# Attention: sums stored ahead of the heads, four places for them, a bfloat16 mask row, reciprocals as 128x16, filler beside the last products

## The chip, the core and the metric

The kernel runs on one core of one Trainium2 chip. A core has a matrix engine (PE, with its weight loads shown apart as PEld), a vector engine (DVE), a scalar engine (ACT), a general engine (POOL), and a queue from which transfers are issued (SP). Each of them works through its own list of instructions in order and waits for semaphores that the others raise. The metric is device microseconds of one execution; the time of a kernel is the median of several executions.

## The reference

One layer of a hybrid decoder block on x of 2048 x 1024 (float32): a root-mean-square norm, one input projection, three mixers that read the same projection, and one output projection that is added to x. The attention mixer is the part that the change touches: 8 heads of 64, causal, with a cumulative forget gate in the exponent.

```python
q = rms_norm(q, q_g); k = rms_norm(k, k_g); c = cumsum(log_f)
logits = q @ k.T * scale + (c_q[:, None] - c_k[None, :])
logits = where(kpos <= qpos, logits, -inf)
p = softmax(logits);  o = p @ v            # per head, then * silu(z_att)
mix = concat([y_att, y_ssd, y_lru])        # 512 + 1024 + 512 columns
h = h + mix @ w_out
```

The other two mixers are a chunked state-space scan (SSD) and a gated linear recurrence (LRU). Products are made to float32 accuracy by splitting each operand into a high and a low part and adding three products.

## The kernel before

**Order.** The program is traced in one order, and a planner then makes the list of every engine from it: it simulates the program and gives an engine, among the instructions whose operands and buffer places are ready in the simulation, the one that stands first in the traced order (a block with `high_priority` counts as traced earlier; `issue_after` keeps a block behind a given instruction). So the traced order is a preference and not the order itself, and a small edit can move many instructions after it. A buffer pool with `bufs=n` has n places for a tag; the next tile of the tag waits until the oldest place has been read.

**Stages.** From 0 to about 1257 us the norm, the projections, the convolutions, the LRU and the SSD run; all results go to DRAM tensors. From there to about 1862 us attention runs (`score`, `av`, `finish`), with pieces of the output projection laid between as filler. After that only output projection is left.

**Attention.** `units` holds 64 pairs (head, block of 256 queries); the first head goes through its blocks downward, the others upward, so that each head from the second on starts with short units. `tasks` holds a unit's key blocks of 256, 288 in all. For task i the loop at L1324 calls `score` (two pairs of products into a PSUM tile T, on the diagonal a mask product; ACT's exponential twice, L1069 and L1070, DVE's difference L1071, POOL's running sum of the exponentials), `av` of task i - 3 (L1114 to L1116, accumulated in O), and, where that ends a unit, `finish`. `maxima` prepares the next unit: row minima of the logits on DVE (L1022 with the mask `zm` on the diagonal chunk, L1027 elsewhere, joined at L1025), which `flip` (L1040 to L1042) puts as a row into q. `load_head` loads a head's keys and values, 2.6 MB.

**What finish does.** Two small products add up the exponentials (L1124, L1125). ACT copies the upper half of O to `to` (L1128) and the row of sums to `su` (L1129, three places), DVE joins `to` (L1130, L1131), POOL multiplies with the gate into `za` (L1132, five places). One task later `store` sends `za` to `at_d` (L1138) and `su` to `s_d` (L1139). After the last head of a block the sums of all 8 heads of 256 positions come back as `sr` of 16 x 128 (L1145, one place), DVE takes the reciprocal (L1146), `r_d` is stored (L1147), and four tasks later the block is marked ready. `later(f, n)` runs f n tasks on.

**Filler.** `sweeps` is a generator over the output projection; a step is three products of 512 columns (L1192 to L1194), four steps are a `half`, which DVE adds to the running result (L1198, L1200). Within attention all halves share one PSUM bank (`psP`). After each `score` the loop calls `fill`, which lets the generator go on to `FIRST + count * RATE // 288` steps, 12 + 290 after the last of 288 tasks, each step behind marks on PE, ACT and DVE four tasks back. In the last three turns of the loop there is no score, so no `fill`. Then the attention's PSUM pools are closed, and the rest of the generator runs with six banks. `mix` loads a block of attention output and the reciprocals (`rb`, L1168).

All these transfers are issued on SP, in one list.

Of the kernel before, what the change touches and what calls it, by code (L numbers as in the profile page):

```python
# [8 lines left out]
F32 = mybir.dt.float32  # L9
F32R = mybir.dt.float32r  # L10
I32 = mybir.dt.int32
BF16 = mybir.dt.bfloat16
# [6 lines left out]
P = 128  # L19
# [19 lines left out]
AVL = 3  # L39
# [10 lines left out]
def hybrid_block(ctx, tc, x, norm_g, w_in, q_norm_g, k_norm_g, forget_b, ssd_conv_w, ssd_conv_b,  # L50
# [3 lines left out]
    def tpool(**kw):  # L54
        if kw.get("space") is not DRAM:
            kw["reuse_waits"] = "tile"
        return tc.tile_pool(**kw)

    V, A, G, T = nc.vector, nc.scalar, nc.gpsimd, nc.tensor
    dma = nc.sync.dma_start  # L60
# [8 lines left out]
    def dram(name, shape, dt=F32):  # L69
        return dp.tile(shape, dt, name=name, tag=name)  # L70
# [12 lines left out]
    s_d = dram("s_d", [NT, 8, P])  # L83
    r_d = dram("r_d", [NT, 8, P])
    gt_d = [dram(f"gt_d{g}", [4, P, S]) for g in range(2)]
    at_d = dram("at_d", [4, P, S])
# [135 lines left out]
    with tpool(name="p0", bufs=2) as p0, tpool(name="p01", bufs=1) as p01, \  # L222
# [81 lines left out]
        for tb in range(4):  # L304
            if tb + AHEAD < 4:
                norm_x(tb + AHEAD)
            for k in range(KD):
                pt, tag = ((psY, "Y"), (pst, "pt"))[(tb * KD + k) % 5 % 2]
# [11 lines left out]
            if tb == 0:  # L320
# [5 lines left out]
                j = CV["cw"]  # L326
                V.tensor_scalar(cv[:, j:j + 60], cv[:, j:j + 60], 0.5, None, op0=ALU.mult)
                j = CV["qg"]
                V.tensor_scalar(cv[:, j:j + 1], cv[:, j:j + 1], -0.125, None, op0=ALU.mult)
                j = CV["ba"]  # L330
                V.tensor_scalar(cv[:, j:j + 4], cv[:, j:j + 4], -1.0, None, op0=ALU.mult)
                j = CV["bx"]
# [180 lines left out]
    with tpool(name="cl", bufs=1) as cl, tpool(name="g1", bufs=1, side="right") as g1:  # L513
        for gq in range(6):
# [5 lines left out]
            if gq == 3:  # L520
                ll = cl.tile([P, 4], F32, name="ll")
                j = CV["lam"]
# [265 lines left out]
    def load_head(h):  # L788
        p, b = divmod(h, 2)
        hs = slice(b * 64, b * 64 + 64)  # L790
        pool = kvB if b else kvA
        k2 = k2s[b]
        kx = pool.tile([P, S], F32R, name=f"kx{h}", tag="kx")

        vv = pool.tile([P, NT, 130], F32R, name=f"vv{h}", tag="vv")
        dma(k2[0:64, :].bitcast(F32), qk_d["k", "h", p][hs, :])
        dma(k2[64:66, :].bitcast(F32), c_d[h].rearrange("i t l -> i (t l)"))
        dma(kx[0:64, :].bitcast(F32), qk_d["k", "l", p][hs, :])
        dma(kx[64:128, :].bitcast(F32), qk_d["k", "h", p][hs, :])
        dma(vv[:, :, 0:128].bitcast(F32), v_d[:, h, :].rearrange("(t p) c -> p t c", p=P))  # L800
        G.memset(vv[:, :, 128:130].bitcast(F32), 1.0)
        heads[h] = k2, kx, vv

    def load_q(j):
        h, sb = units[j]
        p, b = divmod(h, 2)
        hs = slice(b * 64, b * 64 + 64)
        q3, qx = q3s[j // 2 % 3], qxs[j // 2 % 3]
        sb -= sb % 2
        qs = slice(sb * 256, sb * 256 + 512)  # L810
        dma(q3[0:64, :].bitcast(F32), qk_d["q", "h", p][hs, qs])
        dma(qx[0:64, :].bitcast(F32), qk_d["q", "h", p][hs, qs])
        dma(qx[64:128, :].bitcast(F32), qk_d["q", "l", p][hs, qs])
        qs_[j // 2] = q3, qx

    kc = kvA = kvB = zm = onr = idr = zmt = None
# [3 lines left out]
    def make_q(pool):  # L820
        i = len(q3s)
        q3 = pool.tile([P, 512], F32R, name=f"q3{i}")
        G.memset(q3[64:128, :].bitcast(F32), 0.0)
        G.memset(q3[64:66, :].bitcast(F32), 1.0)
        q3s.append(q3)
        qxs.append(pool.tile([P, 512], F32R, name=f"qx{i}"))

    def make_k2(b):
        k2 = (kvB if b else kvA).tile([P, S], F32R, name=f"k2{b}")
        G.memset(k2[64:128, :].bitcast(F32), 0.0)  # L830
        G.memset(k2[96:97, :].bitcast(F32), -1.0)
        k2s[b] = k2

    def begin():

        nonlocal kc, kvA, zm, onr, idr, zmt
        sx.close()
        sgx.close()
        kc = cx.enter_context(tpool(name="kc", bufs=1, side="right"))
        kvA = cx.enter_context(tpool(name="kvA", bufs=1, side="right"))  # L840

        zm = kc.tile([P, 640], F32, name="zm")
        G.memset(zm, 0.0)
        G.affine_select(out=zm[:, 512:640], in_=zm[:, 512:640], pattern=[[-1, P]],
                        compare_op=ALU.is_ge, fill=-NEG, base=0, channel_multiplier=1)

        onr = kc.tile([P, 65], F32R, name="onr")
        G.memset(onr[:, 0:64].bitcast(F32), 0.0)
        G.memset(onr[:, 64:65].bitcast(F32), 1.0)
        idr = kc.tile([P, P], F32R, name="idr")  # L850
        V.tensor_copy(idr, ident)
        zmt = kc.tile([P, P], F32R, name="zmt")
        V.tensor_scalar(zmt, tri, NEG, -NEG, op0=ALU.mult, op1=ALU.add)
        for i in range(2):
            make_q(kc)
        make_k2(0)
        load_head(0)
        load_q(0)
# [111 lines left out]
    a1 = cx.enter_context(tpool(name="a1", bufs=1))  # L970
    a2 = cx.enter_context(tpool(name="a2", bufs=2))
    a3 = cx.enter_context(tpool(name="a3", bufs=3))
    a4 = cx.enter_context(tpool(name="a4", bufs=4))
# [125 lines left out]
    def av(j, kp):  # L1099


        h, sb = units[j]
        u = U[j]
        vv = heads[h][2]
        if kp == 0:
            u["O"] = psO.tile([P, 512], F32, name=f"O{j}", tag="O")
        po = u["O"]
        ph, pl = u.pop(kp)
        for jj in range(2):
            kt = kp * 2 + jj  # L1110
            qs = slice(P if kp == sb and jj else 0, 256)
            cs = slice(256 * jj, 256 * jj + 256 - qs.start)
            q2 = slice(256 + qs.start, 512)
            T.matmul(po[:, qs], vv[:, kt, 0:128], ph[:, cs], start=(kt == 0),  # L1114
                     stop=(kt == 2 * sb + 1), skip_group_check=True)
            T.matmul(po[0:65, q2], vv[:, kt, 64:129], pl[:, cs], start=False, stop=False,  # L1116
                     skip_group_check=True)

    def finish(j):

        h, sb = units[j]
        u = U[j]
        po = u["O"]
        T.matmul(po[0:65, 256:512], onr, u["ah"], start=False, stop=False, skip_group_check=True)  # L1124
        T.matmul(po[0:65, 256:512], onr, u["al"], start=False, stop=True, skip_group_check=True)  # L1125
        to = a2.tile([64, 256], F32, name=f"to{j}", tag="to")
        su = a3.tile([1, 256], F32, name=f"su{j}", tag="su")
        A.copy(to, po[64:128, 0:256])  # L1128
        A.copy(su, po[64:65, 256:512])  # L1129
        V.tensor_tensor(to, po[0:64, 0:256], to, op=ALU.add)  # L1130
        V.tensor_tensor(to, po[0:64, 256:512], to, op=ALU.add)  # L1131
        G.tensor_tensor(u["za"], to, u["za"], op=ALU.mult)  # L1132
        p, b = divmod(h, 2)
        cs = slice(sb * 256, (sb + 1) * 256)
        qt = slice(sb * 2, sb * 2 + 2)

        def store():
            dma(at_d[p][b * 64:b * 64 + 64, cs], u["za"])  # L1138
            dma(s_d[qt, h:h + 1, :].rearrange("i o t -> o i t"),  # L1139
                su.rearrange("o (i t) -> o i t", i=2))  # L1140
            if h < 7:
                return

            sr = a1.tile([16, P], F32, name=f"sr{j}", tag="sr")
            later(lambda: dma(sr, s_d[qt].rearrange("i h t -> (i h) t")), 2)  # L1145
            later(lambda: V.reciprocal(sr, sr), 4)  # L1146
            later(lambda: dma(r_d[qt].rearrange("i h t -> (i h) t"), sr), 5)  # L1147
            later(lambda: ready.add(sb), 8)

        later(store, 1)  # L1150


# [55 lines left out]
    def later(f, n=2):  # L1208

        if clock[0] is None:  # L1210
            f()
        else:
            late.append((clock[0] + n, f))

    def run_late(t):
        clock[0] = t
        while True:
            due = [z for z in late if t is None or z[0] <= t]
            if not due:
                return  # L1220
            due = min(due, key=lambda z: z[0])
            late.remove(due)
            due[1]()
# [80 lines left out]
    def fill(ins):  # L1304
        count[0] += 1
        marks["P"].append(ins)
        want = FIRST + count[0] * RATE // 288
        while want > count[1]:
            with ExitStack() as behind:
                for m in marks.values():  # L1310
                    behind.enter_context(tc.issue_after(m[max(0, len(m) - 1 - LAG)].ins))
                if next(filler):
                    break
            count[1] += 1

    tasks = [(j, kp) for j, (h, sb) in enumerate(units) for kp in range(sb + 1)]
    begin = [tasks.index((j, 0)) for j in range(len(units))]
    at = {}
    for j in range(1, len(units)):
        a, b = max(0, begin[j - 1] - LT), begin[j] - LT  # L1320
# [3 lines left out]
    for i in range(len(tasks) + AVL + 1):  # L1324
        ins = None
        run_late(i)
        if i < len(tasks):
            ins = score(*tasks[i])
            for f in at.get(i, ()):
                f()  # L1330
        if 0 <= i - AVL < len(tasks):
            av(*tasks[i - AVL])
        if i > AVL:
            j, kp = tasks[i - AVL - 1]
            if kp == units[j][1]:
                finish(j)
        if ins is not None:
            fill(ins)
# [36 lines left out]
```

## Time and profile before

| | us |
|---|---|
| median of 3 runs | 2002.28 |
| lowest, highest | 1999.08, 2002.97 |
| profiled execution | 2005.07 |
| its span, first to last instruction | 2003.4 |
| PE busy in the span | 1945.2 |
| DVE, ACT, POOL busy | 1287.7, 1004.3, 804.5 |

The span is what the profile divides up; the profiled execution is 1.7 us longer than it, and 2.8 us above the median of the runs. PE is the engine with the most work by far. A row of the timeline gives start, duration, engine, line and operation, the output and inputs by the program's names, and in brackets how long the engine had been idle and what it waited for. Pipelined products overlap in their records: products of 512 columns start 0.23 us apart at full clock although each is shown with 0.39.

### The profile page before, as it was taken

To read this page: it belongs to the slowest core of one execution; us is meant where nothing else is said; L and a number is where in the kernel's file an instruction comes from. 1 tells how busy PE (TensorE), PEld (TensorE's weight loads), DVE (VectorE), ACT (ScalarE), POOL (GpSimd) and SP (SyncE) were. 2 spreads that over 40 slices of the span, in tenths; PEclk is the share of its full clock that TensorE was granted. 3 is DMA by queue.
4 is the path that set the end of the run, shared out by engine and by line. 5 is a ranking of instruction groups with operands and counts; after the bars stand their busy time and mean duration, and the time that the engine had idled before them with its cause. 6 is when DMAs were issued, how large, how long until landed. Compare 5 with 4: busy or idle time off the path is not lost.

```text
span 2003.4 us, 34852 instructions
## 1 busy us (share of the span) xinstructions
PE 1945.2 (97%) x11941; PEld 1705.6 (85%) x11941; DVE 1287.7 (64%) x2573; ACT 1004.3 (50%) x2174; POOL 804.5 (40%) x920
## 2 busy tenths in 40 slices
PE   8999999999999999999999999999999999998999
PEld 6898888888989899888987897888899788987787
DVE  6738555573736465766566554788788787897433
ACT  6624444362535354444444433576777676775110
POOL 0100000131323233343443520787888688886110
PEclk9999999999999999999999999999999999999999
DMA  5232223111212134657646555764665754722453
GB/s 191 67 116 66 67 69 111 53 55 53 65 43 70 37 103 139 173 177 202 195 147 200 177 135 179 213 174 150 170 164 183 195 154 135 191 64 85 149 173 126
DMA packets 260032, 261.30 MB, mean 130 GB/s; under 512 B 26724, under 2 KB 198016, under 8 KB 258304
## 3 DMA queue, kind: packets, MB, share of 16 engines
q1 hardware_dynamic: 259696, 259.05, 44.1%
q8 instruction: 95, 1.56, 0.3%
q0 software_dynamic: 160, 0.03, 0.1%
q14 instruction: 81, 0.66, 0.1%
HBM read 164.22 MB, written 94.77 MB: 129 GB/s over the span
## 4 chain that ended last, share of the span: by engine, by line
PE 82%; DMA 6%; DVE 6%; ACT 3%; issue 2%; POOL 1%; SPq 1%; DVEq 0%; POOLq 0%; ACTq 0%
PE po L1192 6%; PE po L1194 5%; PE po L1193 5%; PE pxx L372 4%; PE pxx L373 4%; PE pxx L374 4%; PE pzs L358 3%; PE pzs L356 3%; PE pzs L360 3%; PE T L1058 3%; PE T L1059 3%; PE S L1017 3%; PE O L1114 3%; PE O L1116 3%; PE py L727 2%
## 5 line engine op out<-in xcount | busy, mean ns | idle before, releaser
L1071 DVE TENSOR_TENSOR pl<-T,ph 128x512 fp32r<-128x512 f32 (+1 forms) x288 | 185.8, 653 | 44.6 <-ACT T L1070 40.0
L1192 PE MATMUL po<-woh,mh 128*128 128x512 f32 x512 | 204.1, 399 | 0.5 <-DVE xr L1200 0.4
L1193 PE MATMUL po<-wol,mh 128*128 128x512 f32 x512 | 202.2, 395 | 0.0
L1194 PE MATMUL po<-woh,ml 128*128 128x512 f32 x512 | 201.9, 395 | 0.0
L1069 ACT ACTIVATE ph<-T 128x512 fp32r<-128x512 f32 (+1 forms) x288 | 165.4, 574 | 55.9 <-PE T L1059 48.1
L1084 POOL TENSOR_TENSOR ac<-ac,ph 128x512 f32<-128x512 f32 x120 | 157.6, 1313 | 22.5 <-ACT ph L1069 17.6
L1070 ACT ACTIVATE T<-T 128x512 f32<-128x512 f32 (+1 forms) x288 | 164.6, 571 | 0.3
L1058 PE MATMUL T<-q,k 128*128 128x256 f32 x576 | 147.2, 281 | 8.6 <-ACT q L1042 6.6
L356 PE MATMUL pqk<-wh,uh 128*128 128x256 f32 x512 | 155.3, 304 | 0.0
L372 PE MATMUL pxx<-uh,wh 128*128 128x512 f32 x384 | 153.7, 403 | 1.3 <-ACT uh L317 1.3
L373 PE MATMUL pxx<-ul,wh 128*128 128x512 f32 x384 | 153.1, 399 | 0.0
L374 PE MATMUL pxx<-uh,wl 128*128 128x512 f32 x384 | 150.9, 395 | 0.0
L1114 PE MATMUL O<-ph,vv 128*128 128x256 f32 (+1 forms) x576 | 148.6, 279 | 0.7 <-ACT ph L1069 0.7
L1027 DVE TENSOR_REDUCE mc<-S 128x1 f32<-128x512 f32 x192 | 128.5, 682 | 32.4 <-PE S L1017 30.8
L358 PE MATMUL pqk<-wl,uh 128*128 128x256 f32 x512 | 145.1, 284 | 0.8 <-DVE wl L210 0.8
L710 ACT ACTIVATE ab<-ab,nacs 128x128 f32<-128x128 f32 x256 | 82.8, 392 | 125.6 <-POOL ab L706 125.2
L435 DVE SCALAR_TENSOR_TENSOR accx<-rtx,cv,accx 128x512 f32<-128x512 f32 x144 | 108.1, 752 | 57.8 <-ACT accx L432 54.9
L360 PE MATMUL pqk<-wh,ul 128*128 128x256 f32 x512 | 144.2, 282 | 0.0
L358 PE MATMUL pzs<-wl,uh 128*128 128x256 f32 x512 | 143.6, 281 | 0.0
L360 PE MATMUL pzs<-wh,ul 128*128 128x256 f32 x512 | 143.3, 280 | 0.0
L356 PE MATMUL pzs<-wh,uh 128*128 128x256 f32 x512 | 143.0, 281 | 0.0
L1116 PE MATMUL O<-pl,vv 128*65 128x256 f32 x576 | 141.4, 278 | 1.5 <-DVE pl L1071 1.5
(357 smaller groups left out, 5743.3 us busy)
## 6 DMA issues: line engine op xcount, KB each, us to landing
ab<-acs_d SPq DMA_DIRECT2D x64, 256.0 KB
pt_d<-xr SPq DMA_DIRECT2D x64, 256.0 KB
wr<-in_w_in_dram SPq DMA_DIRECT2D x112, 128.0 KB
xt<-in_x_dram SPq DMA_DIRECT2D x16, 512.0 KB
xs_d<-stx SPq DMA_DIRECT2D x32, 256.0 KB
v_d<-vs SPq DMA_DIRECT2D x32, 256.0 KB
wr<-in_w_in_dram SPq DMA_DIRECT2D x128, 64.0 KB
zs_d<-zs SPq DMA_DIRECT2D x32, 256.0 KB
```

The source lines that it names most:

```text
L356: T.matmul(ps[:, i, :], h[k][:, sl], wh[k], start=(k == 0 and i == 0), stop=False, skip_group_check=True)
L358: T.matmul(ps[:, i, :], h[k][:, sl], wl[k], start=False, stop=False, skip_group_check=True)
L360: ins = T.matmul(ps[:, i, :], l[k][:, sl], wh[k], start=False, stop=last, skip_group_check=True)
L372: T.matmul(ps, wh[k][:, ms], uh[tb][k], start=(k == 0), stop=False)
L373: T.matmul(ps, wh[k][:, ms], ul[tb][k], start=False, stop=False)
L374: ins = T.matmul(ps, wl[k][:, ms], uh[tb][k], start=False, stop=(k == KD - 1))
L1058: T.matmul(ps, k2[:, ks], q3[:, qs], start=(jj == 0), stop=False, skip_group_check=True)
L1114: T.matmul(po[:, qs], vv[:, kt, 0:128], ph[:, cs], start=(kt == 0), stop=(kt == 2 * sb + 1), skip_group_check=True)
L1116: T.matmul(po[0:65, q2], vv[:, kt, 64:129], pl[:, cs], start=False, stop=False, skip_group_check=True)
L1192: T.matmul(ps, mh[:, j, :], h, start=(j == 0), stop=False)
L1193: T.matmul(ps, mh[:, j, :], l, start=False, stop=False)
L1194: T.matmul(ps, ml[:, j, :], h, start=False, stop=(j == 3))
```

## The change

The mask `zm` is held in bfloat16. `su` has four places instead of three. `store` sends the sums first, and the head's part `za` one task later than before. The 16 x 128 sums come back as 128 rows of 16, and go back in the same shape. `av` returns its last instruction, so that the last three turns of the loop, which have no score, call `fill` too, with the product's instruction as the mark: 291 calls instead of 288.

```diff
-        zm = kc.tile([P, 640], F32, name="zm")
+        zm = kc.tile([P, 640], BF16, name="zm")
...
-            T.matmul(po[0:65, q2], vv[:, kt, 64:129], pl[:, cs], start=False, stop=False,
-                     skip_group_check=True)
+            ins = T.matmul(po[0:65, q2], vv[:, kt, 64:129], pl[:, cs], start=False, stop=False,
+                           skip_group_check=True)
+        return ins
...
-        su = a3.tile([1, 256], F32, name=f"su{j}", tag="su")
+        su = a4.tile([1, 256], F32, name=f"su{j}", tag="su")
...
+        def flat(z):
+            return z.rearrange("i h (a b) -> (i h a) b", b=16)
+
         def store():
-            dma(at_d[p][b * 64:b * 64 + 64, cs], u["za"])
             dma(s_d[qt, h:h + 1, :].rearrange("i o t -> o i t"),
                 su.rearrange("o (i t) -> o i t", i=2))
+            later(lambda: dma(at_d[p][b * 64:b * 64 + 64, cs], u["za"]), 1)
             if h < 7:
                 return
-            sr = a1.tile([16, P], F32, name=f"sr{j}", tag="sr")
-            later(lambda: dma(sr, s_d[qt].rearrange("i h t -> (i h) t")), 2)
+            sr = a1.tile([P, 16], F32, name=f"sr{j}", tag="sr")
+            later(lambda: dma(sr, flat(s_d[qt])), 2)
             later(lambda: V.reciprocal(sr, sr), 4)
-            later(lambda: dma(r_d[qt].rearrange("i h t -> (i h) t"), sr), 5)
+            later(lambda: dma(flat(r_d[qt]), sr), 5)
...
-            av(*tasks[i - AVL])
+            ins = av(*tasks[i - AVL]) if ins is None else (av(*tasks[i - AVL]), ins)[1]
```

## The prediction

> **What bounds the kernel now.** I read the page's first part, then the table by windows for attention, then the waits and timelines of PE inside it.
>
> ```profile
> PE 1945.2 (97%) x11941; PEld 1705.6 (85%) x11941; DVE 1287.7 (64%) x2573; ACT 1004.3 (50%) x2174; POOL 804.5 (40%) x920
> ```
>
> ```profile
> 1257.30:1862.00 604.70, 586.27 (x3789) 522.39 (x3790) 487.72 (x1137) 420.06 (x956) 474.34 (x523) 0.99 0.55 156
> ...
> 1558.00:1634.00 76.00, 71.67 (x456) 63.70 (x455) 59.48 (x143) 50.92 (x116) 56.22 (x62) 0.96 0.60 165
> 1786.00:1862.00 76.00, 67.17 (x406) 57.88 (x405) 57.96 (x115) 43.48 (x96) 52.99 (x55) 0.96 0.31 91
> ```
>
> The columns are the stretch, its length, busy time with counts of PE, PEld, DVE, ACT, POOL, then granted clock, DMA share and GB/s. PE bounds: it is idle for 604.7 - 586.3 = 18.4 us in attention, the only stage that the change reaches. Of the stretches of one head, that from 1558 and the last one lose 4.3 and 8.8 us and show a lower clock; all others together lose 5.3. No edit removes a product, so the change can only win idle time and halved clock. Three places hold most of it.
>
> The first is at 1570 (PE, ACT and SP by the timeline):
>
> ```profile
> 1574.04 0.58 PE L1058 MATMUL T<-q,k 128*128 128x256 f32 x1 [3.46 <-ACT q L1042]
> 1575.07 0.63 PE L1192 MATMUL po<-woh,mh 128*128 128x512 f32 x1
> ```
>
> ```profile
> 1557.93 0.36 ACT L1129 COPY su<-O 1x256 f32<-1x256 f32 x1
> ...
> 1563.43 0.36 ACT L1129 COPY su<-O 1x256 f32<-1x256 f32 x1
> 1573.08 0.36 ACT L1129 COPY su<-O 1x256 f32<-1x256 f32 x1 [4.18 <-DMA s_d<-su]
> 1573.47 0.26 ACT L1041 CAST q<-T 1x128 fp32r<-1x128 f32 x1
> ```
>
> ```profile
> 1557.62 0.54 SPq L800 DMA_DIRECT2D vv<-v_d  x1
> 1558.26 7.99 SPq L1251 DMA_DIRECT2D pt_d<-xr  x1
> 1568.79 0.60 SPq L1139 DMA_DIRECT2D s_d<-su  x1
> ```
>
> A head's load has filled the transfers; SP is held for 7.99 us by the store behind it, so the sums of three short units wait for their issue. All three places of `su` are full, ACT waits 4.18 us for the first to land, and `flip`'s copies stand behind it, for which PE waits.
>
> The second is the end of attention:
>
> ```profile
> 1854.62 0.33 PE L1116 MATMUL O<-pl,vv 128*65 128x256 f32 x1 [1.27 <-DVE pl L1071]
> 1855.71 0.48 PE L1124 MATMUL O<-ah,onr 128*65 128x256 f32 x1 [0.64 <-ACT ah L1095]
> 1856.51 0.48 PE L1125 MATMUL O<-al,onr 128*65 128x256 f32 x1 [0.33 <-POOL al L1096]
> 1856.79 0.63 PE L1192 MATMUL po<-woh,mh 128*128 128x512 f32 x1
> 1859.25 0.39 PE L1192 MATMUL po<-woh,mh 128*128 128x512 f32 x1
> 1859.94 0.39 PE L1192 MATMUL po<-woh,mh 128*128 128x512 f32 x1
> ```
>
> The third is the chain of sums and reciprocals in the last head (PE, DVE, and the chain of waits):
>
> ```profile
> 1804.76 0.79 PE L1017 MATMUL S<-k,q 96*128 96x512 f32 x1 [2.21 <-DVE mc L1027]
> 1815.01 0.36 PE L1058 MATMUL T<-q,k 128*128 128x256 f32 x1 [1.73 <-DVE mz L1025]
> 1838.23 0.35 PE L1040 MATMUL T<-ident,mz 128*97 128x128 f32 x1 [0.92 <-DVE mz L1025]
> ```
>
> ```profile
> 1802.55 1.56 DVE L1170 TENSOR_TENSOR mt<-mt,rb 128x512 f32<-128x512 f32 x1 [1.53 <-DMA rb<-r_d]
> 1813.38 0.94 DVE L1146 RECIPROCAL sr<-sr 16x128 f32<-16x128 f32 x1 [3.22 <-DMA sr<-s_d]
> 1837.21 0.94 DVE L1146 RECIPROCAL sr<-sr 16x128 f32<-16x128 f32 x1
> ```
>
> Each time DVE waits for a transfer of this chain (1.53, 3.22) or works on a reciprocal (0.94), and the minima for which PE waits stand behind that in DVE's list.
>
> **The price of a halved clock.** After the 3.46 us wait, products of 512 columns take 0.63 instead of 0.39. Two stretches of the table by windows give the clock:
>
> ```profile
> 1574.00:1579.30 5.30, 5.26 (x16) 4.39 (x16) 2.57 (x7) 1.96 (x4) 1.87 (x3) 0.51 0.70 202
> 1856.80:1859.20 2.40, 2.40 (x7) 1.92 (x7) 1.53 (x3) 0.63 (x2) 0.56 (x1) 0.52 0.56 201
> 1804.70:1807.90 3.20, 3.14 (x10) 2.46 (x11) 3.02 (x8) 0.43 (x3) 0.00 (x0) 0.50 0.20 56
> ```
>
> 5.26 us at 0.51 is 2.6 us lost, 2.40 at 0.52 is 1.2, 3.14 at 0.50 is 1.6.
>
> **Part by part.**
>
> *Four places for the sums.* The fourth copy was due at 1573.08 - 4.18 = 1568.9 and finds a place; a fifth would have to come before the first landing at 1573.08, and the units after the short ones are longer. The wait on PE goes, 3.46 + 2.6 = 6.1 us. What is late next: the held SP list, which also carries q loads and gate loads; that is a rival. Bounds: 0 (another wait takes over) and -6.1. I take -6.1, since the row names `su`'s store and nothing else on ACT is due in those 4.18 us.
>
> *Filler beside the last products.* Three more calls make 12 + 291 * 290 // 288 = 305 steps instead of 302. A step takes 1859.94 - 1859.25 = 0.69 us, three 2.07. PE idles 1.27 + 0.64 + 0.33 = 2.24 in those turns and then loses 1.2 at half clock; the products moved there are gone from the full stretch behind. Against it: the planner already reaches over the loop's end.
>
> ```profile
> L1192 PE MATMUL po<-woh,mh 128*128 128x512 f32 x304 | 122.7, 404 | 0.5 <-DVE xr L1200 0.4
> 1852.47 0.67 DVE L1200 TENSOR_TENSOR xo<-xo,po 128x256 f32<-128x256 f32 x2
> ```
>
> Up to 1856.6 it had issued 304 steps, 76 whole halves, though the loop had asked for 302 and begun the last of them: the rest of a half that has its bank can be drawn ahead. The new half needs that bank emptied by DVE first, which ended at 1853.1 (L1200), so it can't start before the waits and lies where PE idles. I take 2.0 of the idle time and half of the clock's price: -2.6. Bounds 0 and -3.4. The Trainium skill, page "TensorE: Matmul & The Clock Gate", section "Why this matters for your kernels", asks for no idle gap above about 3 us, as one idle window halves the clock. Here the clock halved after a gap of 2.21 us and after 2.24 us in three pieces, so the measured rows decide; by the page the tail would be worth 2.0 and the sum would end 0.6 us higher.
>
> *Reciprocals as 128x16.* The rows by shape:
>
> ```profile
> L1146 DVE RECIPROCAL sr<-sr 16x128 f32<-16x128 f32 x8 | 7.5, 940 | 8.7 <-DMA sr<-s_d 8.5
> L144 DVE RECIPROCAL spf_d<-spf_d 128x128 f32<-128x128 f32 x1 | 0.9, 947 | 0.0
> L144 DVE RECIPROCAL spl_d<-spl_d 128x4 f32<-128x4 f32 x1 | 0.2, 178 | 0.0
> ```
>
> The partitions don't count, the elements in a row do: (947 - 178) / 124 = 6.2 ns each, so 16 take 252 ns. DVE wins 8 * 0.69 = 5.5 us. Of the eight only that at 1837.21 stands ahead of an instruction for which PE waits (0.92): -0.7. The others lie beside PE's work. The bounds are 0 and -0.9; if the cover goes, each is worth up to 0.69. Against it stand the transfers: a row of 64 bytes instead of 512. No row here is of this form.
>
> ```profile
> 1804.17 1.52 DMA sr<-s_d
> ...
> 1809.22 2.54 DMA r_d<-sr
> ```
>
> I take the landing as unchanged (1.5 and 2.5 us, mostly fixed: a row of 8 KB takes it); bounds are that and twice that. The Trainium skill, page "DMA: Bandwidth & Descriptors", section "Specifications", says that transfers below 512 bytes per piece fall off line rate and are read and written back; no run here shows it. It is a rival below.
>
> *Sums first, heads one task later.* The two stores of one unit already go in this order, as here:
>
> ```profile
> 1847.99 0.60 SPq L1139 DMA_DIRECT2D s_d<-su  x1
> 1850.02 0.49 SPq L1138 DMA_DIRECT2D at_d<-za  x1
> SPq L1002 <- DMA at_d<-za: 66.2, 45, 5.0
> ```
>
> The heads move by a task, 604.7 / 288 = 2.1 us. They hold one of five places of `za`, and SP waits for such a store in front of the next gate load already 45 times. Behind a waiting gate load stand q loads and sums. I take 0, since the gate is needed only in `finish`, units later; bounds 0 and the slower rival. The reads of `at_d` are let go only at the mark eight tasks on, which the new time doesn't reach.
>
> *Mask in bfloat16.* 128 instructions read it.
>
> ```profile
> L1022 DVE CUSTOM_DVE_ANT_0 jk<-S,zm 128x512 bf16<-128x512 f32 x32 | 21.9, 685 | 3.4 <-PE S L1017 2.4
> L1027 DVE TENSOR_REDUCE mc<-S 128x1 f32<-128x512 f32 x192 | 128.5, 682 | 32.4 <-PE S L1017 30.8
> ```
>
> The reduction without a mask takes as long, so the second operand costs nothing now: 0, bounded by 128 * 3 ns either way on DVE.
>
> *New order.* The planner lays attention out anew. The waits of 2.21 and 1.73 and a dozen under 0.7 are accidents of its order; some will go and others come. As an allowance I charge one new wait of the middle size, +1.7; bounds: -5.5 (2.21 + 1.6 + 1.73 gone) and +5.5 (as much again).
>
> **The sum.** 2003.4 - 6.1 - 2.6 - 0.7 + 1.7 = 1995.7 of span, 1997.4 with the 1.7 us around it, against 2005.07 of the same execution: 0.9962. On the median of the runs, 2002.28, that is 1994.6; I say 1995.
>
> **The rivals.**
>
> *Another wait takes the sums' place.* SP stays held for 7.99 us, and ACT, freed, meets the next thing that waits on it. For it: every head's load does this. Against: no other PE wait near 1570 names a transfer. The first term goes, 1995 + 6 = 2001.
>
> *The filler is drawn ahead.* The change then doesn't do what it says: as with the 304 steps, the planner places the steps before the waits, and the end stays as it is. 1995 + 2.6 = 1997.6.
>
> *Small pieces lengthen the sums' chain.* `sr` has one place, so each load waits for the last `r_d` to land (2.54, then 1.52). Twice that in the fast units at 1788 to 1815 would stretch the two waits of 2.21 and 1.73 by as much and halve the clock once: +4 to +6, about 2000. For it: SP has just this wait there. Against: 8 KB is little beside 91 GB/s in that head.
>
> *Chain's waits go too.* A shorter reciprocal and sums stored ahead take the 5.5 us at 1802 and 1815 with them: 1995 - 5.5 - 1 = 1988.5.
>
> *Slower: places of the gate.* Heads stored 2.1 us later hold `za`'s five places at the short units; the gate load stands at the head of SP's list, and q loads behind it come late. It decides where the lag exceeds the time that q loads have in hand; where they have none, a head's start costs 2.1 us and 1.6 at half clock. At four of the seven heads that begin with short units that is 4 * 3.7 = 14.8, about 2010. For it speak the 66.2 us that SP waits so already; against it, that no PE wait shown here names a transfer.
>
> **How the numbers follow.** Forecast 0.38, another wait 0.22, filler ahead 0.10, small pieces 0.08, chain's waits gone 0.10, slower 0.12. A measurement tells about 0.2%, 4 us, from no change: 1998.3 to 2006.3 counts as the same. Faster: 0.38 + 0.10 + 0.07 of the filler case = 0.55; same: 0.22 + 0.08 + 0.03 = 0.33; slower 0.12. The range leaves out the slower case and the outer edges of the first and fourth rivals: 1988 to 2004.
>
> **What would show it.** `su` no longer waits for `s_d<-su` on ACT, and no PE wait above 1 us stands at a head's start; filler products lie between the last `av` and the sums' products, at full clock; L1146 falls to about 0.25 us; L1022 keeps 685 ns; s_d stands ahead of at_d as before. The prediction is wrong if PE's idle time in attention stays near 18 us: then the planner's order, not these places, sets it.

## The result, and the profile after

The changed kernel takes 1988.33 us as the median of 6 runs, beside 2000.68 us for the kernel before (6 runs): ratio 0.9941, 95% interval 0.9923 to 0.996, so 8 to 15 us less. The forecast was 1995, by its sum a ratio of 0.9962; the time lies just inside the low end of its range. The profiled execution took 1992.75 us, its span 1990.9.

First the page of the kernel after, then its table by windows (the stretch, its length, busy time of PE, PEld, DVE, ACT and POOL with counts, granted clock, DMA share, GB/s).

```profile
span 1990.9 us, 34851 instructions
...
PE 1937.7 (97%) x11941; PEld 1699.0 (85%) x11941; DVE 1283.9 (64%) x2573; ACT 1003.7 (50%) x2174; POOL 804.4 (40%) x920
```

```profile
1256.10:1852.00 595.90, 586.04 (x3805) 523.46 (x3806) 485.40 (x1139) 420.39 (x957) 474.34 (x524) 1.00 0.56 158
...
1556.00:1632.00 76.00, 74.28 (x488) 66.51 (x489) 63.46 (x153) 55.30 (x128) 60.38 (x68) 1.00 0.67 181
...
1780.00:1852.00 72.00, 68.83 (x424) 60.60 (x423) 55.82 (x119) 44.33 (x98) 53.33 (x56) 0.98 0.34 97
```

PE's idle time in attention is 595.9 - 586.0 = 9.9 us, where it was 18.4; the head at 1556 has the full clock, where it had 0.96. To see where the time went I take the same instructions of PE in both traces as marks, before and then after (the row at 1838.23, the last mark of before, stands in the prediction):

```profile
1556.67 0.47 PE L1017 MATMUL S<-k,q 96*128 96x512 f32 x1 [0.50 <-DMA q<-qh_d]
1600.38 0.49 PE L1017 MATMUL S<-k,q 96*128 96x512 f32 x1 [0.24 <-DVE mc L1027]
1793.93 0.39 PE L1058 MATMUL T<-q,k 128*128 128x256 f32 x1 [0.52 <-ACT q L1042]
```

```profile
1556.88 0.47 PE L1017 MATMUL S<-k,q 96*128 96x512 f32 x1 [1.17 <-DMA q<-qh_d]
1594.48 0.50 PE L1017 MATMUL S<-k,q 96*128 96x512 f32 x1 [0.25 <-DVE mc L1027]
1788.26 0.39 PE L1058 MATMUL T<-q,k 128*128 128x256 f32 x1 [0.16 <-ACT q L1042]
1798.73 0.51 PE L1196 MATMUL po<-woh,mh 128*128 128x512 f32 x1 [2.03 <-ACT mh L1175]
1828.72 0.35 PE L1040 MATMUL T<-ident,mz 128*97 128x128 f32 x1 [0.21 <-DVE mz L1025]
1846.95 0.40 PE L1196 MATMUL po<-woh,mh 128*128 128x512 f32 x1
```

- From 1556 on: 1600.38 - 1556.67 = 43.71 us before, 1594.48 - 1556.88 = 37.60 after: **-6.1**, the wait for the sums' places with its half clock.
- From there to the flip in the last head: 1838.23 - 1600.38 = 237.85 and 1828.72 - 1594.48 = 234.24: **-3.6**, for the same 1,490 products of PE. The mark at the start of the last head (1793.93 and 1788.26) divides it into 193.55 and 44.30 before, 193.78 and 40.46 after, but the changed list has some products ahead of this mark that stood behind it, so only the two together compare like with like. The waits of 2.21 and 1.73 are gone; one of 2.03, ahead of a filler product, has come.
- The end: from 1828.72 to 1846.95 it takes 18.2 us until all products of attention and 308 filler steps are done. Before, from 1838.23, it took 22.4 (304 steps by 1856.6, then four more, by 1860.6 in its timeline): **-4.2**.
- The rest of the span differs by +1.4: -1.2 ahead of the first unit, +1.4 from there to 1556, and +1.2 behind PE's last product, where 5.0 us pass before the span ends instead of 3.9.

The rows that answer to the first place, ACT and SP of the kernel after:

```profile
1558.12 0.36 ACT L1130 COPY su<-O 1x256 f32<-1x256 f32 x1
1561.91 0.36 ACT L1130 COPY su<-O 1x256 f32<-1x256 f32 x1
...
1563.63 0.36 ACT L1130 COPY su<-O 1x256 f32<-1x256 f32 x1
1568.99 0.36 ACT L1130 COPY su<-O 1x256 f32<-1x256 f32 x1
1569.93 0.26 ACT L1041 CAST q<-T 1x128 fp32r<-1x128 f32 x1 [0.57 <-PE T L1040]
```

```profile
1558.31 7.63 SPq L1255 DMA_DIRECT2D pt_d<-xr  x1
...
1569.61 0.60 SPq L1142 DMA_DIRECT2D s_d<-su  x1
```

SP is held as long as before (7.63 us beside 7.99), and the first of the four sums isn't sent before 1569.61. But the fourth copy, at 1568.99, has its place, and ACT goes on. The sums do not leave earlier; they wait where nobody stands behind them.

The end, PE of the kernel after:

```profile
1843.48 0.28 PE L1116 MATMUL O<-pl,vv 128*65 128x256 f32 x1
1843.60 0.40 PE L1196 MATMUL po<-woh,mh 128*128 128x512 f32 x1
...
1846.12 0.39 PE L1198 MATMUL po<-woh,ml 128*128 128x512 f32 x1
1846.35 0.28 PE L1114 MATMUL O<-ph,vv 128*128 128x256 f32 x1
...
1846.70 0.29 PE L1125 MATMUL O<-ah,onr 128*65 128x256 f32 x1
```

Where the three waits were, a whole half of filler lies, twelve products from 1843.60 to 1846.35, and the last products of attention follow at full clock, without a wait in brackets.

### The profile page after: what moved, and what is told of

Same layout as the page of the kernel before. It is cut to its first block, busy times and chain, and to the rows that moved or that the text cites. A ratio compares the mean times of both kernels' runs of the same rounds, so it can differ in the third digit from the quotient of the medians.

```text
span 1990.9 us, 34851 instructions
## 1 busy us (share of the span) xinstructions
PE 1937.7 (97%) x11941; PEld 1699.0 (85%) x11941; DVE 1283.9 (64%) x2573; ACT 1003.7 (50%) x2174; POOL 804.4 (40%) x920
## 3 DMA queue, kind: packets, MB, share of 16 engines
q1 hardware_dynamic: 261488, 259.05, 44.1%
## 4 chain that ended last, share of the span: by engine, by line
PE 83%; DMA 5%; DVE 5%; ACT 3%; issue 2%; SPq 1%; POOL 1%; DVEq 0%; POOLq 0%; ACTq 0%
PE po L1196 6%; PE po L1198 6%; PE po L1197 6%; PE pxx L373 4%; PE pxx L372 4%; PE pxx L374 4%; PE T L1058 3%; PE T L1059 3%; PE pzs L358 3%; PE pzs L356 3%; PE pzs L360 3%; PE O L1114 3%; PE S L1017 3%; PE O L1116 3%; PE pqk L358 2%; PE pqk L356 2%
## 5 line engine op out<-in xcount | busy, mean ns | idle before, releaser
L1059 PE MATMUL T<-qx,kx 128*128 128x256 f32 x576 | 143.8, 281 | 0.0
```

What stands on the lines that cost most here:

```text
L1059: ins = T.matmul(ps, kx[:, ks], qx[:, qs], start=False, stop=True, skip_group_check=True)
```

## The experiments

My theory: the parts act singly, each on its own wait. The rivals: the gain comes from a new order of the lists; or from the sums being stored first; or another wait takes the place of each that goes. The table compares the order in which the instructions stand in each run's trace with that of the kernel before, line numbers left out. It counts the fewest instructions that must be moved, or have another shape, to turn one list into the other (on SP, transfers that must be moved):

```
                    PE   DVE  ACT  POOL  SP
four places, mask    0    0    0    2     0
filler               6    2    0    0     0
reciprocals         16   18    0    0    11
stores' order        0    0    0    0     2
whole change        22   20    0    2    13
```

The two on POOL prepare the mask and only have another type. Of PE's 11,941 instructions the whole change leaves the first 10,980 in their order; the next stands in the last head. On PE, DVE and ACT seven heads keep their order.

**Four places for the sums, with the mask in bfloat16, whose smaller row makes room for them.**

```diff
-        zm = kc.tile([P, 640], F32, name="zm")
+        zm = kc.tile([P, 640], BF16, name="zm")
-        su = a3.tile([1, 256], F32, name=f"su{j}", tag="su")
+        su = a4.tile([1, 256], F32, name=f"su{j}", tag="su")
```

> The kernel before with four places for the sums and the bfloat16 mask that makes room for them, nothing else. The lists of all engines stay instruction for instruction those of before, so only the wait can differ. Theory 'places': the 4.18 us wait of ACT at a head's start and the 3.46 us of PE behind it go, with 2.6 us at half clock: -6.1 us, ratio 0.997. Rival 'held queue': ACT meets another wait behind the held SP list, 0 to -2 us. Rival 'stores': sums wait because at_d stands before s_d in the traced order, so a place more gives nothing: 0.

Ratio 0.9967 (0.9954 to 0.998), -6.6 us of 1997.7. In its timeline PE has no wait above 0.7 us between 1245 and 1780, and ACT none for `s_d<-su`. The first theory held. No other wait of that size came, the stores kept their order, and with equal lists a new order is excluded.

**Filler beside the last products.** `av` returns its last instruction, and the loop passes it on:

```diff
-            av(*tasks[i - AVL])
+            ins = av(*tasks[i - AVL]) if ins is None else (av(*tasks[i - AVL]), ins)[1]
```

> The kernel before with the three more filler calls beside the last products, nothing else. Theory 'filler': the waits of 1.27, 0.64 and 0.33 us at the end of attention go and the clock stays full there: -3.4 us, ratio 0.9983. Rival 'drawn ahead': the planner places the steps before the last scores, 0.

Ratio 0.9984 (0.997 to 0.9997), -3.2 us. PE of this run, at the head's start and at the end:

```profile
1569.36 0.39 PE L1058 MATMUL T<-q,k 128*128 128x256 f32 x1 [3.09 <-ACT q L1042]
...
1845.53 0.47 PE L1193 MATMUL po<-woh,mh 128*128 128x512 f32 x1 [0.19 <-DVE xo L1201]
...
1848.34 0.28 PE L1114 MATMUL O<-ph,vv 128*128 128x256 f32 x1
```

The steps were not drawn ahead: they wait 0.19 us for the bank to be emptied (xo, L1201), and fill the place of the three waits up to 1848.34. The wait for the sums' places (3.09) is there still.

**Sums and reciprocals as 128 rows of 16.** With both transfers of `sr` in that shape:

```diff
-            sr = a1.tile([16, P], F32, name=f"sr{j}", tag="sr")
+            sr = a1.tile([P, 16], F32, name=f"sr{j}", tag="sr")
```

> The kernel before with the sums and reciprocals as 128 rows of 16, nothing else. Theory 'short on DVE': L1146 falls to 0.25 us and the waits of PE behind it in the last head shrink, -0.7 us by the prediction, -3.8 us by the profile after (from 1838.23 - 1793.93 = 44.30 to 1828.72 - 1788.26 = 40.46). Rival 'small pieces': rows of 64 bytes take longer to land, the load is later than 1.5 us and the waits grow: +2 or more.

Ratio 0.9992 (0.9977 to 1.0006), -1.6 us: told apart neither from nothing nor from -0.7 or -3.8. The profiles say more. First three of PE's waits in the last head with the long reciprocal, from the filler's run:

```profile
1796.40 0.50 PE L1017 MATMUL S<-k,q 96*128 96x512 f32 x1 [0.90 <-DVE mc L1027]
1799.38 0.35 PE L1040 MATMUL T<-ident,mz 128*97 128x128 f32 x1 [1.53 <-DVE mz L1025]
1830.35 0.35 PE L1040 MATMUL T<-ident,mz 128*97 128x128 f32 x1 [0.77 <-DVE mz L1025]
```

All waits above 0.45 us in the last head, ahead of its end, come to 4.3 us there, 4.8 in the run of the places, 5.3 in that of the stores' order and 6.0 in the profile of before, all four with one and the same list. With the short reciprocal they are 2.03 and 0.61, 2.6 us. By these waits the edit is worth 1.7 to 3.4 us.

The time between two instructions counts smaller waits and the clock as well. From the mark at 1600.38 to the flip at 1838.23 PE does the same 1,490 products in every run. That takes 237.1 to 237.9 us in the four profiles with the long reciprocal, and 232.4 to 234.3 in the five with the short one (this run, the kernel after, and the runs of the reciprocal's duration, of three places and of two places for `sr`, below). The means differ by 3.7 us, and the -3.6 of the first pair was no exception.

**Only the duration of the reciprocal**, on the kernel before:

```diff
-            later(lambda: V.reciprocal(sr, sr), 4)
+            later(lambda: V.reciprocal(sr[:, 0:16], sr[:, 0:16]), 4)
```

> The kernel before, in which the reciprocal covers only the first 16 of the 128 columns of the 16 x 128 sums (the rest goes back unchanged, so most of the output of the attention is left undivided); the transfers keep rows of 512 bytes. The lists of PE, DVE and ACT are those of the run with 128 rows of 16. Theory 'short on DVE': the time on DVE and the list that follows from it are what counts, so this gives the same as that run, 0.999 and the waits of PE in the last head near 2.6 us instead of 4.3 to 6. Rival 'shape of the transfers': rows of 64 bytes cost or win something of their own, then the two differ by 2 us or more and by the landing of sr and r_d.

Ratio 0.999 (0.9977 to 1.0002), or -2.0 us of 1999.65, as the run before it. DVE by shape, first of the run with 128 rows, then of this one, with PE's wait in its last head:

```profile
L1149 DVE RECIPROCAL sr<-sr 128x16 f32<-128x16 f32 x8 | 1.9, 242 | 5.2 <-DMA sr<-s_d 5.2
```

```profile
L1146 DVE RECIPROCAL sr<-sr 16x16 f32<-16x16 f32 x8 | 1.9, 235 | 5.7 <-DMA sr<-s_d 5.7
```

```profile
1802.49 0.51 PE L1192 MATMUL po<-woh,mh 128*128 128x512 f32 x1 [2.03 <-ACT mh L1171]
```

DVE waits 5.2 us for the sums with rows of 64 bytes and 5.7 with rows of 512, and PE's waits are the same. The shape of the transfers costs nothing that these runs show; what the edit does goes through the time on DVE and the lists that are planned from it, which are the same in both runs. Time and lists were not taken apart, so for this part of the gain a new order is not excluded.

**The order of the stores.**

```diff
-            dma(at_d[p][b * 64:b * 64 + 64, cs], u["za"])
             dma(s_d[qt, h:h + 1, :].rearrange("i o t -> o i t"),
                 su.rearrange("o (i t) -> o i t", i=2))
+            later(lambda: dma(at_d[p][b * 64:b * 64 + 64, cs], u["za"]), 1)
```

> The kernel before with the sums' store traced first and the heads' store one task later, nothing else. In the planned lists only three transfers on SP change places (a gate load and a store move ahead of a q load). Theory: 0 within 0.1%, at worst the 0.5 us wait of PE for a q load grows to the 1.2 us of the kernel after. Rival 'stores': the sums go earlier and the 4.18 us wait of ACT goes: -6 us. Rival 'places of the gate': later heads hold the gate's places and q loads are late: +3 us or more.

Ratio 0.9997 (0.9982 to 1.0012): no difference found. ACT and PE wait as before:

```profile
1568.79 0.36 ACT L1129 COPY su<-O 1x256 f32<-1x256 f32 x1 [3.75 <-DMA s_d<-su]
```

```profile
1569.76 0.58 PE L1058 MATMUL T<-q,k 128*128 128x256 f32 x1 [3.04 <-ACT q L1042]
...
1571.21 0.63 PE L1193 MATMUL po<-wol,mh 128*128 128x512 f32 x1
```

PE's wait for a q load near 1553 (0.50 before) is 1.13 us here, but 1.15 and 1.05 in the runs of the filler and of the reciprocals too, whose SP lists are unchanged there: it varies by itself.

**The change with three places.**

```diff
-        su = a4.tile([1, 256], F32, name=f"su{j}", tag="su")
+        su = a3.tile([1, 256], F32, name=f"su{j}", tag="su")
```

> The changed kernel with three places for the sums again; all lists stay those of the changed kernel. Theory 'places': ACT waits some 4 us for the landing of a sum at the head's start near 1568 again and PE some 3 us behind it, +6 us against the changed kernel, ratio to the kernel before 0.997. Rival 'stores': with the sums stored first the places don't matter, ratio 0.994 as the changed kernel.

Ratio 0.9959 (0.9945 to 0.9973) to the kernel before, 0.0018 or 3.6 us above that of the change. ACT and PE of this run:

```profile
1574.34 0.36 ACT L1130 COPY su<-O 1x256 f32<-1x256 f32 x1 [4.28 <-DMA s_d<-su]
```

```profile
1575.30 0.58 PE L1058 MATMUL T<-q,k 128*128 128x256 f32 x1 [3.56 <-ACT q L1042]
```

The wait is back although the sums are stored first and the mask has its narrow row, so it is the fourth place that counts. The time is less than the 6 us that I expected; the intervals of this run and of the change overlap, and the size stays open between these. In the profiles the stretch of the first place (1556.67 to 1600.38 in the kernel before) takes 44.1 us here and 37.6 in the kernel after, 6.5 more; but the profiled execution, 2000.06 us, was the slowest of this run's twelve.

**Two places for `sr`**, on the changed kernel, an attempt at the wait of 2.03.

```diff
-            sr = a1.tile([P, 16], F32, name=f"sr{j}", tag="sr")
+            sr = a2.tile([P, 16], F32, name=f"sr{j}", tag="sr")
```

> The changed kernel with two places for sr, so that the load of the next sums doesn't wait for the store of the last reciprocals to land. If the wait of 2.03 us on PE near 1799 comes from that chain, it goes: -2 to -3.7 us against the changed kernel, ratio 0.9925. Rival 'queue': SP's list order sets it, the wait stays or moves, ratio 0.994.

Ratio 0.9941 (0.9926 to 0.9956), the same as the change. PE and DVE of this run:

```profile
1794.47 0.47 PE L1116 MATMUL O<-pl,vv 128*65 128x256 f32 x1 [1.98 <-DVE mz L1025]
```

```profile
1792.32 1.49 DVE L1174 TENSOR_TENSOR mt<-mt,rb 128x512 f32<-128x512 f32 x1 [0.86 <-DMA rb<-r_d]
```

The wait has moved and not gone. DVE still waits for the reciprocals' way back through DRAM (`rb<-r_d`) shortly ahead of it.

## Why the prediction was right, and where its sizes were off

| term, us | predicted | pair of profiles | nine profiles | run alone (interval) |
|---|---|---|---|---|
| four places, with the mask | -6.1 | -6.1 | -4.8 | -6.6 (-9.2 to -4.0) |
| filler | -2.6 | -4.2 | -3.9 | -3.2 (-6.0 to -0.6) |
| reciprocals | -0.7 | -3.6 | -3.7 | -1.6 (-4.6 to +1.2) |
| stores' order | 0 | | | -0.6 (-3.6 to +2.4) |
| new order, allowance | +1.7 | | | |
| elsewhere | | +1.4 | | |
| sum | -7.7 | -12.5 | -12.4 | -12.0 |

The last column is (ratio - 1) * 1997.7, the median of before beside these runs. Its parts add up to what the whole change gave, 0.0059 * 2000.68 = 11.8 us, but each has an interval of some 5 us. The column ahead of it takes PE's time between the same marks in all nine profiles, and the mean of those with an edit less the mean of those without:

- From 1556.67 to 1600.38: 40.4 to 44.1 us in six profiles with three places, 37.5 to 37.6 in three with four.
- From 1600.38 to 1838.23: 237.1 to 237.9 in four with the long reciprocal, 232.4 to 234.3 in five with the short one.
- From 1838.23 until all products of attention and 308 filler steps are done: 21.1 to 22.5 in five without the filler calls, 18.2 to 18.6 in four with them.

*Four places.* Right in place and mechanism. The held SP list, the first rival, was there (7.63 us) and took nothing back: no other wait above 0.7 us came in that stretch. The size fits the pair of profiles exactly because both numbers come from one execution of before; over six profiles the wait cost 2.9 to 6.5 us. One of the prediction's signs did not come: a PE wait above 1 us still stands at this head's start, the 1.17 for a q load. It isn't the change's, as it varies with the list unchanged.

*Filler.* Right that it fills the waits and isn't drawn ahead, because the new half needs an emptied bank. The size was cut too far. Of the 4.2 us, 2.3 are idle time (3.0 before, 0.8 after), and 1.9 are products at a slower clock (0.92 in this stretch before, 1.00 after), of which I had charged 0.6. That price is not paid each time: the run of the stores' order went through the same three waits, 2.34 us in all, at full clock, and took 21.1.

*Reciprocals.* The duration was predicted at 252 ns and is 245. The row of the kernel after:

```profile
L1150 DVE RECIPROCAL sr<-sr 128x16 f32<-128x16 f32 x8 | 2.0, 245 | 3.4 <-DMA sr<-s_d 3.2
```

But the term counted one reciprocal on the path and took the others as covered by PE's work. This is where the sum went furthest wrong: 0.7 was charged, and the stretch shows 3.7. The prediction's own rows held a second one. The reciprocal that starts at 1813.38 ends 0.94 us later, and the minima for which PE waits 1.73 us at 1815.01 stand right behind it, with one instruction between:

```profile
1814.80 0.13 DVE L1025 TENSOR_REDUCE mz<-mc 128x1 f32<-128x4 f32 x1
```

With it the term would have been about 1.4. Whether the rest comes from the shorter time at the other reciprocals or from the lists that were planned from it stays open. The rival of the small pieces fell.

*Stores' order and mask.* Nothing, as said. The instruction with the mask kept its time:

```profile
L1022 DVE CUSTOM_DVE_ANT_0 jk<-S,zm 128x512 bf16<-128x512 f32 x32 | 21.9, 685 | 3.3 <-PE S L1017 2.2
SPq L1002 <- DMA at_d<-za: 65.7, 44, 5.4
```

The second row, from SP's waits, shows the gate loads behind the heads' stores: 65.7 us in 44 cases, 66.2 in 45 before. No wait of PE shows that the later heads held anything up, and no run gave the slower rival ground.

*The allowance for a new order* is a step that failed as reasoning. I wrote that the planner lays attention out anew. It did not: seven heads kept their lists on PE, DVE and ACT, and what moved lies in the last head and at the end, where a duration and the steps changed. There the new order came with a gain and not with a price. Without the +1.7 the sum is -9.4. The +1.4 elsewhere is no price of moved work on PE: the stretch from the first unit to 1556 took from 298.9 to 300.8 us in nine profiles with one and the same list of PE, and the 1.2 at the end lies behind PE's last product.

*The chain's waits go too*: this rival came half true. Those of 2.21 and 1.73 went, and one of 2.03 came. It had a chance of 0.10, and its 1988.5 is what carried the range down to 1988. That the measured 1988.33 lies inside is in part luck: the forecast itself was 6.7 us off, of which 1.6 is the median of before, 2000.68 in the six runs and 2002.28 in the three that I started from.

## What to carry to other kernels

A wait for a small tile's place can cost far more than its transfer when the engine that waits has the next stage's input behind it: look at what stands there, and give the tile one more place, before trying to speed up the queue that holds it. Before charging an edit for a new order, compare the planned lists; here more places and a narrower mask changed none of them, while a shorter instruction did. And a price read from one pair of profiles holds that execution's luck: one and the same list gave waits of 4.3 to 6.0 us in four profiles. The time between the same two instructions, taken in every profile at hand, spread less than the difference that was sought.

## What the runs showed of the hardware that was not expected

Whether a wait of this length halves the clock did not follow from its length. The same wait at the same instruction was followed by half clock in the run of the stores' order (3.04 us of waiting, products at 0.63) and by full clock in that of the filler (3.09 us). The table by windows, first the filler's run, then the stores' order's; the clock is the third number from the end:

```profile
1569.30:1572.70 3.40, 3.34 (x19) 2.96 (x20) 2.58 (x7) 1.93 (x6) 1.89 (x3) 1.00 0.65 199
```

```profile
1569.30:1572.70 3.40, 2.94 (x9) 2.55 (x10) 2.86 (x8) 2.35 (x6) 1.81 (x3) 0.51 0.75 219
```

The Trainium skill, page "TensorE: Matmul & The Clock Gate", section "What's actually happening", says that the window over which activity is judged runs freely, not from the program's start; these two rows agree with that.

Of the six profiles with this wait, four show a clock of 0.50 to 0.58 behind it (waits of 3.04, 3.35, 3.46 and 3.56 us) and two a clock of 1.00 (2.55 and 3.09 us). At the end of attention the clock was lower in four of the five profiles without the filler calls: after 1.92 us of waiting in three pieces products took 0.63 us in the run of the reciprocals, and after 2.34 us they took 0.40 in that of the stores' order.

I take it that a term for half clock is best charged as a chance times its size. The 2.6 us that I charged in full for the first place were nothing in two of six executions, and the runs alone, -6.6 with an interval of 5 us, can't tell the two.
